# A streaming mean reduction: the first tile loaded by two DMAs, split by partitions

## The chip, the cores and the metric

The kernel runs on one core of one Trainium2 chip. The metric is the device time of one execution in microseconds. Every execution quoted here was with a granted clock of 1.00. Executions of one kernel agree within about 0.1%, so a difference of 1 us in 1246 can be read from medians, and one of 0.2 us can't.

Three words are used throughout. A *tile* is 8 MB of the input, 128 partitions with 65,536 bytes each. A *row* is the 65,536 bytes of one partition; in the trace it is one packet of one of the core's 16 DMA engines. A *piece* is one of the two DMAs that load the first tile after the change.

## The reference

```python
def setup_inputs():
    return {"x": np.random.randn(64, 256, 8192).astype(np.float32)}

def reference(x):
    return np.mean(x, axis=2)
```

That is 537 MB of input, read once, and 64 KB of output. The arithmetic is one addition for each element.

## The kernel before

The input is 16,384 vectors of 8192 floats. Two of them go to one partition and make a row in the sense above (the expectations below call the same thing, as it is read from memory, a row pair). 63 tiles go through three buffers in turn; the rest is loaded as one half tile and four column chunks. SyncE issues all loads. It issues tile t only when VectorE has reduced tile t-3. The first three loads are moved ahead of the start barrier.

```python
R = 2; NP = 63; NBUF = 3; P = 128; L = 8192
x_pair = x_rows.rearrange("(t p r) l -> t p (r l)", p=P, r=R)
bufs = [E(nc.sbuf_tensor(f"buf{i}", [P, R * L], f32)) for i in range(NBUF)]
in_sems = [E(nc.semaphore(f"in_sem{i}")) for i in range(NBUF)]
# ... cut: small buffers, other semaphores
def sync_program(eng):
    for t in range(NP):
        if t >= NBUF:
            eng.wait_ge(dve_sem, t - NBUF + 1)
        eng.dma_start(bufs[t % NBUF][:], x_pair[t]).then_inc(in_sems[t % NBUF], 16)
    # ... cut: the half tile, four column chunks, the stores

def vector_program(eng):
    def pair(k, trip, dst):
        eng.wait_ge(in_sems[k], trip)
        eng.tensor_reduce(dst, bufs[k][:].rearrange("p (r l) -> p r l", r=R), X, ADD
        ).then_inc(dve_sem, 1)
    with eng.Fori(0, trips) as i:
        for k in range(NBUF):
            pair(k, 16 * i + 16, res[:, bass.ds(NBUF * i + k, 1), :])
    # ... cut: the last tiles, and the sums that end the kernel
```

Of the kernel before, what the change touches and what calls it, by code (L numbers as in the profile page):

```python
# [6 lines left out]
def bass_global_avg_pool_1d_kernel(  # L7
# [4 lines left out]
    P = 128  # L12
# [14 lines left out]
    NBUF = 3  # L27
# [14 lines left out]
    with ExitStack() as ctx:  # L42
        E = ctx.enter_context
        bufs = [E(nc.sbuf_tensor(f"buf{i}", [P, R * L], f32)) for i in range(NBUF)]
        res = E(nc.sbuf_tensor("res", [P, NP, R], f32))
        res1 = E(nc.sbuf_tensor("res1", [P, 2], f32))
        part = E(nc.sbuf_tensor("part", [P, 8], f32))
        fin = E(nc.sbuf_tensor("fin", [P, 32], f32))
        fint = E(nc.sbuf_tensor("fint", [P, 32], f32))
        ident = E(nc.sbuf_tensor("ident", [P, P], f32))  # L50
        outsb = E(nc.sbuf_tensor("outsb", [NP, P, R], f32))
        out1sb = E(nc.sbuf_tensor("out1sb", [1, P], f32))
        ps = [E(nc.psum_tensor(f"ps{r}", [NP, P], f32)) for r in range(R)]
        psone = E(nc.psum_tensor("psone", [1, P], f32))

        in_sems = [E(nc.semaphore(f"in_sem{i}")) for i in range(NBUF)]
        one_sem = E(nc.semaphore("one_sem"))
        ch_sems = [E(nc.semaphore(f"ch_sem{i}")) for i in range(NCH)]
        dve_sem = E(nc.semaphore("dve_sem"))
        act_sem = E(nc.semaphore("act_sem"))  # L60
        prep_sem = E(nc.semaphore("prep_sem"))
        pe_sem = E(nc.semaphore("pe_sem"))
        cp_sem = E(nc.semaphore("cp_sem"))
        fin_sem = E(nc.semaphore("fin_sem"))
        out_sems = [E(nc.semaphore(f"out_sem{i}")) for i in range(3)]

        b1 = NP % NBUF
        b2 = (NP + 1) % NBUF
        buf1 = bufs[b1]
        buf2 = bufs[b2]  # L70
        offs = [sum(CH[:i]) for i in range(NCH)]
        s0 = CH[0] // 2 - L // 64
        s1 = CH[1] // 2

        def gpsimd_program(eng):
            eng.memset(fin[:], 0.0).then_inc(prep_sem, 1)  # L76
            eng.memset(ident[:], 0.0).then_inc(prep_sem, 1)  # L77
            eng.wait_ge(prep_sem, 2)
            eng.affine_select(  # L79
                out=ident[:],  # L80
                in_=ident[:],
                compare_op=mybir.AluOpType.not_equal,
                fill=1.0,
                base=0,
                pattern=[[-1, P]],
                channel_multiplier=1,
            ).then_inc(prep_sem, 1)

        first = len(nc.main_func.blocks[0].instructions)

        def sync_program(eng):
            for t in range(NP):
                if t >= NBUF:
                    eng.wait_ge(dve_sem, t - NBUF + 1)
                eng.dma_start(bufs[t % NBUF][:], x_pair[t]).then_inc(in_sems[t % NBUF], 16)  # L95
            eng.wait_ge(dve_sem, NP - NBUF + 1)
            eng.dma_start(buf1[:, :L], x_one[T1]).then_inc(one_sem, 16)
            eng.wait_ge(dve_sem, NP - NBUF + 2)
            for c in range(NCH):
                sl = slice(offs[c], offs[c] + CH[c])  # L100
                eng.dma_start(buf2[:, sl], x_one[T2][:, sl]).then_inc(ch_sems[c], 16)  # L101

            eng.wait_ge(cp_sem, 2)
            eng.dma_start(out_pair[0:NP, :], outsb[:].rearrange("t p r -> t (p r)")).then_inc(
                out_sems[0], 16
            )
            eng.wait_ge(cp_sem, 3)
            eng.dma_start(out_one[T1 : T1 + 1, :], out1sb[:]).then_inc(out_sems[1], 16)
            eng.wait_ge(fin_sem, 3)
            eng.dma_start(out_q[4 * T2 : 4 * T2 + 4, :], fint[0:P:32, :]).then_inc(  # L110
                out_sems[2], 16
            )
            for s in out_sems:
                eng.wait_ge(s, 16)
# [6 lines that stand above are left out]
                eng.tensor_reduce(  # L121
                    dst, bufs[k][:].rearrange("p (r l) -> p r l", r=R), X, ADD
                ).then_inc(dve_sem, 1)

            trips = (NP - 1) // NBUF
            with eng.Fori(0, trips) as i:
                for k in range(NBUF):
                    pair(k, 16 * i + 16, res[:, bass.ds(NBUF * i + k, 1), :])
            for t in range(trips * NBUF, NP - 1):
                pair(t % NBUF, 16 * (t // NBUF + 1), res[:, t, :])  # L130
            t = NP - 1
            eng.wait_ge(in_sems[t % NBUF], 16 * (t // NBUF + 1))
            eng.tensor_reduce(res[:, t, 0:1], bufs[t % NBUF][:, :L], X, ADD).then_inc(dve_sem, 1)  # L133
            eng.wait_ge(one_sem, 16)
            eng.tensor_reduce(res1[:, 0:1], buf1[:, : L // 2], X, ADD).then_inc(dve_sem, 1)  # L135
            eng.wait_ge(ch_sems[0], 16)
            eng.tensor_reduce(part[:, 0:1], buf2[:, :s0], X, ADD).then_inc(dve_sem, 1)  # L137
            eng.wait_ge(ch_sems[1], 16)
            eng.tensor_reduce(  # L139
                part[:, 1:2], buf2[:, offs[1] : offs[1] + s1], X, ADD  # L140
            ).then_inc(dve_sem, 1)
            eng.wait_ge(ch_sems[3], 16)
            eng.tensor_reduce(  # L143
                part[:, 2:3], buf2[:, offs[3] : offs[3] + CH[3]], X, ADD
            ).then_inc(dve_sem, 1)
            eng.wait_ge(dve_sem, NP + 4)
            eng.wait_ge(act_sem, 5)
            eng.wait_ge(prep_sem, 1)
            eng.tensor_reduce(fin[:, 0:1], part[:, 0:6], X, ADD).then_inc(fin_sem, 1)  # L149
            eng.wait_ge(fin_sem, 1)  # L150
            eng.transpose(fint[:], fin[:]).then_inc(fin_sem, 1)  # L151
            eng.wait_ge(fin_sem, 2)
            eng.tensor_scalar(  # L153
                fint[:], fint[:], inv, None, mybir.AluOpType.mult
            ).then_inc(fin_sem, 1)

        def scalar_program(eng):
            def acc(dst, src):
                eng.activation(src, src, Copy, accum_out=dst).then_inc(act_sem, 1)  # L159

            t = NP - 1
            eng.wait_ge(in_sems[t % NBUF], 16 * (t // NBUF + 1))
            acc(res[:, t, 1:2], bufs[t % NBUF][:, L:])
            eng.wait_ge(one_sem, 16)
            acc(res1[:, 1:2], buf1[:, L // 2 : L])

            for r in range(R):
                eng.wait_ge(pe_sem, r + 1)
                eng.activation(outsb[:, :, r], ps[r][:], Copy, scale=inv).then_inc(cp_sem, 1)  # L169
            eng.wait_ge(pe_sem, 3)  # L170
            eng.activation(out1sb[:], psone[:], Copy, scale=inv).then_inc(cp_sem, 1)  # L171
            eng.wait_ge(ch_sems[0], 16)
            acc(part[:, 3:4], buf2[:, s0 : CH[0]])
            eng.wait_ge(ch_sems[1], 16)
            acc(part[:, 4:5], buf2[:, offs[1] + s1 : offs[1] + CH[1]])
            eng.wait_ge(ch_sems[2], 16)
            acc(part[:, 5:6], buf2[:, offs[2] : offs[2] + CH[2]])

        def tensor_program(eng):
            eng.wait_ge(prep_sem, 3)  # L180
            eng.wait_ge(dve_sem, NP)
            eng.wait_ge(act_sem, 1)
            for r in range(R):
                eng.transpose(ps[r][:], res[:, :, r], ident[:]).then_inc(pe_sem, 1)  # L184
            eng.wait_ge(dve_sem, NP + 1)
            eng.wait_ge(act_sem, 2)
            eng.matmul(psone[:], res1[:, 0:1], ident[:], start=True, stop=False)  # L187
            eng.matmul(psone[:], res1[:, 1:2], ident[:], start=False, stop=True).then_inc(pe_sem, 1)  # L188

        sync_program(nc.sync)  # L190
        gpsimd_program(nc.gpsimd)
        vector_program(nc.vector)
        scalar_program(nc.scalar)
        tensor_program(nc.tensor)



        stream = nc.main_func.blocks[0].instructions
        loads = stream[first : first + NBUF]
        del stream[first : first + NBUF]  # L200
        at = next(
            i
            for i, ins in enumerate(stream)
            if ins.engine == mybir.EngineType.SP and type(ins).__name__ == "InstDrain"
        )
        stream[at:at] = loads
# [28 lines left out]
```

## Time and profile before

| | before |
|---|---|
| time, median of 3 | 1246.21 us (1245.99 to 1246.72) |
| DMA engines busy | 99.8% of the span |
| rate over the span | 431 GB/s |
| VectorE busy | 87% |
| one reduction of a tile | 17.22 us |
| one row on one DMA engine | 2.418 us, which is 27.1 GB/s |

These lines are from the page of the kernel before: the span; the busy share of the DMA engines in 40 slices, in tenths; what they moved in each slice; the DMA queue with packets, MB and share of 16 engines; the shares of the chain that ended last; and the costliest group of instructions, with its busy time, the mean of one in ns, and the idle time before it.

```profile
span 1244.7 us, 315 instructions
...
DMA  9999999999999999999999999999999999999998
GB/s 436 415 430 438 438 438 438 430 413 438 438 438 438 438 436 411 434 438 438 438 438 438 425 417 438 438 438 438 438 432 411 438 438 438 438 438 436 417 428 373
...
q1 hardware_dynamic: 9874, 536.94, 99.8%
...
DMA 70%; DVE 29%; issue 0%; SPq 0%; DVEq 0%
...
L121 DVE TENSOR_REDUCE res<-buf 128x16384 f32 (+1 forms) x62 | 1067.6, 17220 | 152.3 <-DMA buf<-in_x_dram 152.3
```

The DMA engines are busy 99.8% of the span, and VectorE waits 152.3 us in total for landings. The chain of work that ended last names VectorE for 29%, because each load is issued when a reduction ends, but in that wait the engines have other loads queued and stay busy (99.8%). Two lines of the timeline of VectorE before show the rhythm (start, duration, instruction, and in brackets the idle time before it and what ended it):

```profile
22.14 17.22 DVE L121 TENSOR_REDUCE res<-buf 128x16384 f32 x1 [22.14 <-DMA buf<-in_x_dram]
41.46 17.22 DVE L121 TENSOR_REDUCE res<-buf 128x16384 f32 x1 [2.10 <-DMA buf<-in_x_dram]
```

A tile arrives every 19.3 us, and VectorE is done with the last one 2.1 us earlier. When reduction t ends and tile t+3 is issued, the engines still have 2 us of tile t+1 and all of tile t+2 before them, about 21 us of queued work.

The packets of the trace can be joined into chains, because on each engine a packet starts where the one before ended. Before the change there are 16 such chains. They start between 1.04 and 1.94 us. Their first rows take 2.55 to 3.20 us, and after that practically every full row takes 2.42 us.

### The profile page before, as it was taken

Reading aid. Unit: us, or ns where it says so; the run is one execution under the profiler, and the core shown is the slowest. Engines: PE = TensorE matmul, PEld = TensorE weight load, DVE = VectorE, ACT = ScalarE, POOL = GpSimd, SP = SyncE. Lnnn points to the kernel's source line nnn. Section 1 sums busy time; section 2 is a strip of 40 time slices with the busy share of each in tenths; the row PEclk is TensorE's granted clock in tenths of the full one; section 3 lists DMA queues with packets and bytes.
Section 4 is the critical chain, followed back from the end, with each engine's and each line's share of the span. In section 5 each row is a group of like instructions: output and inputs, shape, how many; then the busy total and the mean of one; then the engine's idle time right before and its main releaser. Section 6 shows DMA issues by size and latency. Waiting matters only on the chain.

```text
span 1244.7 us, 315 instructions
## 1 busy us (share of the span) xinstructions
PE 1.7 (0%) x6; PEld 0.6 (0%) x6; DVE 1085.6 (87%) x70; ACT 17.2 (1%) x14; POOL 0.8 (0%) x7
## 2 busy tenths in 40 slices
PE   0000000000000000000000000000000000000000
PEld 0000000000000000000000000000000000000000
DVE  2898988989889889898898988989889898898897
ACT  0000000000000000000000000000000000000005
POOL 0000000000000000000000000000000000000000
DMA  9999999999999999999999999999999999999998
GB/s 436 415 430 438 438 438 438 430 413 438 438 438 438 438 436 411 434 438 438 438 438 438 425 417 438 438 438 438 438 432 411 438 438 438 438 438 436 417 428 373
DMA packets 9874, 536.94 MB, mean 431 GB/s; under 512 B 1106, under 2 KB 1170, under 8 KB 1426
## 3 DMA queue, kind: packets, MB, share of 16 engines
q1 hardware_dynamic: 9874, 536.94, 99.8%
HBM read 536.87 MB, written 0.07 MB: 431 GB/s over the span
## 4 chain that ended last, share of the span: by engine, by line
DMA 70%; DVE 29%; issue 0%; SPq 0%; DVEq 0%
DMA buf<-in_x_dram 70%; DVE res L121 29%; DVEq L121 0%; SPq L101 0%; DVE part L143 0%; SPq L95 0%; DVE fint L151 0%; DVE fint L153 0%; DVE fin L149 0%
## 5 line engine op out<-in xcount | busy, mean ns | idle before, releaser
L121 DVE TENSOR_REDUCE res<-buf 128x16384 f32 (+1 forms) x62 | 1067.6, 17220 | 152.3 <-DMA buf<-in_x_dram 152.3
L159 ACT ACTIVATE buf<-buf 128x1024 f32<-128x1024 f32 (+3 forms) x5 | 15.0, 2994 | 1221.7 <-DMA buf<-in_x_dram 1221.6
L133 DVE TENSOR_REDUCE res<-buf 128x1 f32<-128x8192 f32 x1 | 8.7, 8685 | 2.1 <-DMA buf<-in_x_dram 2.1
L135 DVE TENSOR_REDUCE res<-buf 128x1 f32<-128x4096 f32 x1 | 4.4, 4419 | 1.0 <-DMA buf<-in_x_dram 1.0
L137 DVE TENSOR_REDUCE part<-buf 128x1 f32<-128x2176 f32 x1 | 2.4, 2421 | 1.1 <-DMA buf<-in_x_dram 1.1
L184 PE MATMUL ps<-ident,res 128*63 128x128 f32 x2 | 0.7, 434 | 1230.8 <-DVE res L133 1230.8
L159 ACT ACT_TABLE_LOAD x1 | 1.3, 1283 | 1.8 <-PEq L220 1.8
L143 DVE TENSOR_REDUCE part<-buf 128x1 f32<-128x512 f32 x1 | 0.7, 686 | 0.7 <-DMA buf<-in_x_dram 0.7
L139 DVE TENSOR_REDUCE part<-buf 128x1 f32<-128x1024 f32 x1 | 1.2, 1220 | 0.1
L159 ACT ACTIVATION_READ_ACCUMULATOR buf<-buf 128x1 f32 x5 | 0.9, 186 | 0.0
L184 PEld LDWEIGHTS ps<-ident,res 128*63 128x63 f32 x2 | 0.3, 202 | 1230.8 <-issue 1230.8
L188 PE MATMUL psone<-ident,res 128*1 128x128 f32 x2 | 0.6, 421 | 0.0
L187 PE MATMUL psone<-ident,res 128*1 128x128 f32 x2 | 0.6, 397 | 4.7 <-DVE res L135 4.7
L169 ACT ACTIVATE outsb<-ps 63x128 f32<-63x128 f32 x2 | 0.4, 264 | 0.0
L79 POOL TENSOR_SCALAR_AFFINE_SELECT ident<-ident 128x128 f32<-128x128 f32 x1 | 0.3, 292 | 0.2 <-POOL ident L77 0.2
L171 ACT ACTIVATE out1sb<-psone 1x128 f32<-1x128 f32 x1 | 0.3, 266 | 1.5 <-PE psone L188 1.5
L188 PEld LDWEIGHTS psone<-ident,res 128*1 128x1 f32 x2 | 0.3, 128 | 0.2
L151 DVE STREAM_TRANSPOSE fint<-fin 128x32 f32<-128x32 f32 x1 | 0.2, 212 | 0.0
L153 DVE TENSOR_SCALAR fint<-fint 128x32 f32<-128x32 f32 x1 | 0.2, 181 | 0.0
L77 POOL MEMSET ident<- 128x128 f32 x1 | 0.2, 204 | 0.0
L149 DVE TENSOR_REDUCE fin<-part 128x1 f32<-128x6 f32 x1 | 0.2, 159 | 0.0
L76 POOL MEMSET fin<- 128x32 f32 x1 | 0.1, 125 | 1.3 <-POOLq L220 1.3
(5 smaller groups left out, 0.5 us busy)
## 6 DMA issues: line engine op xcount, KB each, us to landing
buf<-in_x_dram SPq DMA_DIRECT2D x1, 4096.0 KB, 31.1
buf<-in_x_dram SPq DMA_DIRECT2D x1, 2304.0 KB, 17.3
buf<-in_x_dram SPq DMA_DIRECT2D x1, 1024.0 KB, 19.4
buf<-in_x_dram SPq DMA_DIRECT2D x63, 40.7
buf<-in_x_dram SPq DMA_DIRECT2D x1, 512.0 KB, 20.2
buf<-in_x_dram SPq DMA_DIRECT2D x1, 256.0 KB, 20.4
out_dram<-outsb SPq DMA_DIRECT2D x1, 63.0 KB
out_dram<-out1sb SPq DMA_DIRECT2D x1, 0.5 KB
```

The costliest lines, as they stand in the source:

```text
L79: eng.affine_select(out=ident[:], in_=ident[:], compare_op=mybir.AluOpType.not_equal, fill=1.0, base=0, pattern=[[-1, P]], channel_multipl ...
L121: eng.tensor_reduce(dst, bufs[k][:].rearrange("p (r l) -> p r l", r=R), X, ADD).then_inc(dve_sem, 1)
L133: eng.tensor_reduce(res[:, t, 0:1], bufs[t % NBUF][:, :L], X, ADD).then_inc(dve_sem, 1)
L135: eng.tensor_reduce(res1[:, 0:1], buf1[:, : L // 2], X, ADD).then_inc(dve_sem, 1)
L137: eng.tensor_reduce(part[:, 0:1], buf2[:, :s0], X, ADD).then_inc(dve_sem, 1)
L139: eng.tensor_reduce(part[:, 1:2], buf2[:, offs[1] : offs[1] + s1], X, ADD).then_inc(dve_sem, 1)
L143: eng.tensor_reduce(part[:, 2:3], buf2[:, offs[3] : offs[3] + CH[3]], X, ADD).then_inc(dve_sem, 1)
L159: eng.activation(src, src, Copy, accum_out=dst).then_inc(act_sem, 1)
L169: eng.activation(outsb[:, :, r], ps[r][:], Copy, scale=inv).then_inc(cp_sem, 1)
L184: eng.transpose(ps[r][:], res[:, :, r], ident[:]).then_inc(pe_sem, 1)
L187: eng.matmul(psone[:], res1[:, 0:1], ident[:], start=True, stop=False)
L188: eng.matmul(psone[:], res1[:, 1:2], ident[:], start=False, stop=True).then_inc(pe_sem, 1)
```

## The change

The intent: a small first DMA might get the engines going sooner than one over 128 partitions. The first tile is loaded as partitions 0 to 15 (1 MB) and then 16 to 127 (7 MB). Both pieces count up the same semaphore, so the waits on buffer 0 ask for 16 more.

```diff
+        def landed(t):
+            return 16 * (t // NBUF + 1 + (t % NBUF == 0))
...
-                eng.dma_start(bufs[t % NBUF][:], x_pair[t]).then_inc(in_sems[t % NBUF], 16)
+                for ps in (slice(0, 16), slice(16, P)) if t == 0 else (slice(0, P),):
+                    eng.dma_start(bufs[t % NBUF][ps], x_pair[t][ps]).then_inc(
+                        in_sems[t % NBUF], 16
+                    )
...
-                    pair(k, 16 * i + 16, res[:, bass.ds(NBUF * i + k, 1), :])
+                    pair(k, 16 * i + landed(k), res[:, bass.ds(NBUF * i + k, 1), :])
...  (the other waits on in_sems likewise; NBUF + 1 loads are moved ahead of the barrier)
```

More of the change, by code (lines that the diff above doesn't have):

```diff
@@ L127, in vector_program @@
                 for k in range(NBUF):
-                    pair(k, 16 * i + 16, res[:, bass.ds(NBUF * i + k, 1), :])
+                    pair(k, 16 * i + landed(k), res[:, bass.ds(NBUF * i + k, 1), :])
             for t in range(trips * NBUF, NP - 1):
-                pair(t % NBUF, 16 * (t // NBUF + 1), res[:, t, :])
+                pair(t % NBUF, landed(t), res[:, t, :])
             t = NP - 1
-            eng.wait_ge(in_sems[t % NBUF], 16 * (t // NBUF + 1))
+            eng.wait_ge(in_sems[t % NBUF], landed(t))
             eng.tensor_reduce(res[:, t, 0:1], bufs[t % NBUF][:, :L], X, ADD).then_inc(dve_sem, 1)
@@ L161, in scalar_program @@
             t = NP - 1
-            eng.wait_ge(in_sems[t % NBUF], 16 * (t // NBUF + 1))
+            eng.wait_ge(in_sems[t % NBUF], landed(t))
             acc(res[:, t, 1:2], bufs[t % NBUF][:, L:])
@@ L198, in bass_global_avg_pool_1d_kernel @@
         stream = nc.main_func.blocks[0].instructions
-        loads = stream[first : first + NBUF]
-        del stream[first : first + NBUF]
+        loads = stream[first : first + NBUF + 1]
+        del stream[first : first + NBUF + 1]
         at = next(
```

## The prediction

> **What bounds it now.** The load stream. The page gives DMA 99.8% busy over 16 engines and 431 GB/s over the 1244.7 us span; DVE is busy 87% and waits for landings. In the packets of the trace a full row (65,536 B) takes 2.418 us on an engine (27.1 GB/s), and each engine's next packet starts when its last ends: 16 unbroken chains from 1.04-1.94 us (first packets, 2.5 to 3.2 us each) to the last load's semaphore at 1241.6 us. An 8 MB tile is 8 rows per engine, 19.3 us. A tile's reduction takes 17.22 us. The issue of tile t+3 comes at the end of reduction t, about 2 us before tile t+1 lands, with all of tile t+2 queued: about 21 us of slack. So only time lost or saved by the slowest DMA engine counts, and it counts one for one.
>
> **What the change adds and removes.** It adds one DMA issue (0.41 us each at the start, hidden behind rows of 2.4 us), a register instruction per trip of DVE's loop (DVE waits about 2 us per tile: free) and a wait for 32 instead of 16. Its hope is that a 16-row DMA starts the engines sooner: the first packets start over 0.9 us, so at most that can be won, more likely 0 to 0.5 us.
>
> **The cost I expect.** [...] both pieces still use 16 engines: 16 = 16x1 rows, 112 = 16x7. [...] The trace before has only 128-partition loads, each engine at its full rate, so no run here shows this yet. [...] With jitter in the starts, both pieces together cost the slowest engine 13 to 18 us.
> [...]
>
> Tile 0 lands at about 37 us instead of 22 us. Its reduction and the issue of tile 3 come about 15 us later, inside the 21 us of slack, so nothing starves; but the lost DMA time is never won back. The whole loss is on the critical path.
>
> **Prediction.** 1260 us, 80% range 1250 to 1270. Faster by over 2%: 0.01; within 2%: 0.87; slower by over 2%: 0.12.
>
> **What would show it.** First-row packets of about 9 to 10 us instead of 3; packets of 2.4 to 10 us in the second piece; 2.418 us rows from tile 1 on; DVE's first wait about 37 us instead of 22.1; low GB/s in the first of the 40 slices; steady period unchanged at 19.35 us; the landings of one tile spread over several us (0.75 us before), lasting to the end; the DMA share below 99.8% or unchanged with longer packets.
>
> **What would make it wrong.** [...] a landing later than the 21 us of slack: up to some 1275. Skew between engines that makes later tiles collide would cost more.

The forecast's sum came to 13 to 18 us for both pieces on the slowest engine, and so from the 1246 us of before to 1260 us. The terms of that sum, one for each piece, rested on a model of how the partitions of a piece slow its rows, which no trace or run shows.

## The result, and the profile after

| | before | after |
|---|---|---|
| time, median of 4 | 1246.31 us | 1267.28 us (1266.93 to 1268.19) |
| ratio, after over before | | 1.0169 (95% interval 1.0152 to 1.0187) |
| first reduction starts | 22.14 us | 44.49 us |
| mean rate | 431 GB/s | 424 GB/s |
| DMA engines busy | 99.8% | 99.7% |

Ratios here are the mean time of one kernel's fast runs over that of the other's of the same rounds, so not quite the ratio of the medians that are quoted. The change costs 21 us, 1.7%, clear of noise. The profiled execution was the slowest of the four (1268.19 us), and its span is 22.1 us longer than that of before (1266.8 against 1244.7); the decomposition below belongs to it.

The page after:

```profile
span 1266.8 us, 336 instructions
...
DMA  9999999999999999999999999999999999999997
GB/s 223 348 441 437 433 433 430 430 430 430 430 433 441 445 433 433 433 430 430 430 430 430 435 439 447 430 435 430 430 430 430 430 430 433 445 443 430 435 430 337
...
q1 hardware_dynamic: 9890, 536.94, 99.7%
...
L128 DVE TENSOR_REDUCE res<-buf 128x16384 f32 (+1 forms) x62 | 1067.6, 17220 | 174.4 <-DMA buf<-in_x_dram 174.4
```

The busy digits are as before. What is new is in the line of GB/s: 223 and 348 in the first two slices. The engines read as busy and moved half of what they had moved before in the first slice, and some four fifths in the second. VectorE's reductions take what they took, and its idle time is 22.1 us longer (174.4 against 152.3), which is the whole difference of the spans. Its timeline after shows that all of it is one wait:

```profile
44.49 17.22 DVE L128 TENSOR_REDUCE res<-buf 128x16384 f32 x1 [44.49 <-DMA buf<-in_x_dram]
63.83 17.22 DVE L128 TENSOR_REDUCE res<-buf 128x16384 f32 x1 [2.11 <-DMA buf<-in_x_dram]
83.18 17.22 DVE L128 TENSOR_REDUCE res<-buf 128x16384 f32 x1 [2.13 <-DMA buf<-in_x_dram]
```

The same three stretches of both kernels follow, first before and then after (the stretch in us; busy time of PE, PEld, DVE, ACT and POOL with counts of instructions; the clock; the share of the DMA engines; GB/s). A packet counts where it starts, so a share can pass 1.

```profile
1.00:12.00 11.00, 0.00 (x0) 0.00 (x0) 0.00 (x0) 1.28 (x1) 0.56 (x3) 1.00 1.15 477
12.00:44.00 32.00, 0.00 (x0) 0.00 (x0) 19.76 (x2) 0.00 (x0) 0.00 (x0) 1.00 0.98 426
44.00:64.00 20.00, 0.00 (x0) 0.00 (x0) 17.86 (x2) 0.00 (x0) 0.00 (x0) 1.00 0.97 419
```

```profile
1.00:12.00 11.00, 0.00 (x0) 0.00 (x0) 0.00 (x0) 1.28 (x1) 0.56 (x3) 1.00 1.28 191
12.00:44.00 32.00, 0.00 (x0) 0.00 (x0) 0.00 (x0) 0.00 (x0) 0.00 (x0) 1.00 0.93 238
44.00:64.00 20.00, 0.00 (x0) 0.00 (x0) 17.39 (x2) 0.00 (x0) 0.00 (x0) 1.00 1.04 449
```

The rate falls to 191 and 238 GB/s and is back in the third stretch. Because a packet counts where it starts, these figures are too high for the pieces themselves: the first stretch also counts the first rows of piece 2, and the second counts rows of tile 1. From the starts and ends of the rows below, piece 1 moved its 1 MB in 9.4 us, which is 111 GB/s, and piece 2 its 112 rows in 32.8 us, 224 GB/s. The rows themselves, from the packets of the trace, joined into one chain for each engine (durations in us over the 16 engines; "last end" is when the last engine ended that row):

```
                  before                          after
row of the chain  min  median  max   last end     min  median  max   last end
1                 2.55  3.06  3.20     4.74       7.92  8.66  9.16    10.44   piece 1
2                 2.42  2.42  2.42     7.16       5.22  5.31  5.89    15.66   piece 2
3                 2.42  2.42  2.42     9.57       4.71  4.72  4.80    20.37
4                 2.42  2.42  2.42    11.99       2.96  3.07  4.84    25.20
5                 2.42  2.42  2.42    14.41       3.62  3.62  4.48    28.94
6                 2.42  2.42  2.42    16.82       4.29  4.57  4.76    33.63
7                 2.42  2.42  2.42    19.24       4.70  4.76  4.87    38.38
8                 2.42  2.42  2.42    21.66       4.52  4.57  4.89    43.26
9 (tile 1)        2.42  2.42  2.42    24.08       2.82  3.39  3.67    46.20
```

The sum closes. After piece 1 the last engine is 5.7 us behind (10.44 - 4.74). Piece 2 adds 15.9 us (43.26 - 10.44 is 32.8 us, against 21.66 - 4.74 = 16.9). The first row of tile 1 adds 0.5 us (2.94 against 2.42). 5.7 + 15.9 + 0.5 = 22.1 us, the difference of the spans. The engines started as they had before, at 1.02 to 1.82 us, so the hoped-for gain is not there. From row 10 on every row takes 2.42 us in the median again.

### The profile page after: what moved, and what is told of

It reads as the page before. It is cut to its first block, busy times and chain, and to the rows that moved or that the text cites. A ratio compares the mean times of both kernels' runs of the same rounds, so it can differ in the third digit from the quotient of the medians.

```text
span 1266.8 us, 336 instructions
## 1 busy us (share of the span) xinstructions
PE 1.7 (0%) x6; PEld 0.6 (0%) x6; DVE 1085.6 (86%) x70; ACT 17.2 (1%) x14; POOL 0.8 (0%) x7
## 3 DMA queue, kind: packets, MB, share of 16 engines
q1 hardware_dynamic: 9890, 536.94, 99.7%
## 4 chain that ended last, share of the span: by engine, by line
DMA 69%; DVE 29%; another core or an unknown queue 2%; issue 0%; SPq 0%; DVEq 0%
DMA buf<-in_x_dram 69%; DVE res L128 29%; DVEq L128 0%; SPq L108 0%; DVE part L150 0%; SPq L100 0%; DVE fint L158 0%; DVE fint L160 0%; DVE fin L156 0%
## 5 line engine op out<-in xcount | busy, mean ns | idle before, releaser
L128 DVE TENSOR_REDUCE res<-buf 128x16384 f32 (+1 forms) x62 | 1067.6, 17220 | 174.4 <-DMA buf<-in_x_dram 174.4
```

## The experiments

The theory (A): which partitions a load writes sets how long its rows take. Over all 128 partitions a row takes 2.42 us; in piece 1 of the change it took 8.66 us in the median, in piece 2 from 3.07 to 5.31. In its plain form A says that only the rows that get in each other's way are slow; in the form A2 they hold up the other engines too. The sizes that the expectations give for A come from an estimate; its terms no run here shows. The rivals: a second DMA costs this whatever its shape (B); only the start of the program is sensitive (C); the addresses read in HBM do it, not the partitions written (D); any load below 128 partitions is slow (E).

All runs gave correct results. The median differences below are against the kernel before in the same rounds.

### 1. Two DMAs, split by columns

```diff
-                for ps in (slice(0, 16), slice(16, P)) if t == 0 else (slice(0, P),):
-                    eng.dma_start(bufs[t % NBUF][ps], x_pair[t][ps]).then_inc(
+                for cs in (slice(0, 2048), slice(2048, R * L)) if t == 0 else (slice(0, R * L),):
+                    eng.dma_start(bufs[t % NBUF][:, cs], x_pair[t][:, cs]).then_inc(
```

> The first tile is again loaded by two DMAs of 1 MB and 7 MB with the same semaphore counts, but both cover all 128 partitions: columns 0 to 2047 and then 2048 to 16383. Theory A [...]: no loss, 1245.8 to 1246.8 us, rows of tile 1 at 2.42 us as before, landing of tile 0 near 22 us. Rival B (a second DMA, its issue, the doubled semaphore count or the later loop register work costs the 21 us, whatever the shape): 1262 us or more, tile 0 landing near 44 us.

Measured: 1245.89 us against 1246.07, ratio 0.9998 (0.9985 to 1.0012). VectorE's timeline in this run starts as before:

```profile
22.19 17.22 DVE L128 TENSOR_REDUCE res<-buf 128x16384 f32 x1 [22.19 <-DMA buf<-in_x_dram]
41.54 17.22 DVE L128 TENSOR_REDUCE res<-buf 128x16384 f32 x1 [2.13 <-DMA buf<-in_x_dram]
```

The same two sizes, the same extra issue, the same semaphore counts and the same code on VectorE, and no loss. (The packets differ: one of piece 1 is 8 KB here, as each partition gets 2048 floats; the page counts 10018 in all, against 9874 before.) B falls. This is also the repair: a load that must be split can be split by columns.

### 2. The same split, at tile 60

```diff
-                for ps in (slice(0, 16), slice(16, P)) if t == 0 else (slice(0, P),):
+                for ps in (slice(0, 16), slice(16, P)) if t == 60 else (slice(0, P),):
-            return 16 * (t // NBUF + 1 + (t % NBUF == 0))
+            return 16 * (t // NBUF + 1 + (t == 60))
...  (cut: three loads instead of four are moved ahead of the barrier)
```

> Tile 0 is loaded whole; tile 60 is loaded as partitions 0 to 15 and then 16 to 127. Theory A [...]: about the same loss as at tile 0, 1263 to 1268 us, with rows slowed only in tile 60. Rival C (the loss belongs to the start: a cold DMA queue, or VectorE starting 22 us later and never catching up): below 1250 us, because DVE has nothing to start late for there.

Measured: 1268.85 us, 22.8 us over before (ratio 1.018), slightly above the range expected. The wait is now late in VectorE's timeline, 23.55 us before tile 60, and 1.5 us more than usual before tile 59, which landed while the small piece of tile 60 was being loaded:

```profile
1145.24 17.22 DVE L128 TENSOR_REDUCE res<-buf 128x16384 f32 x1 [2.13 <-DMA buf<-in_x_dram]
1166.03 17.22 DVE L128 TENSOR_REDUCE res<-buf 128x16384 f32 x1 [3.58 <-DMA buf<-in_x_dram]
1206.81 17.22 DVE L128 TENSOR_REDUCE res<-buf 128x2 f32<-128x16384 f32 x1 [23.55 <-DMA buf<-in_x_dram]
```

The rows of that tile repeat the pattern of the change: 8.64, 5.29, 4.78, 2.94, 4.11, 4.57, 4.76, 4.39 us in the median. C falls. VectorE's late start at tile 0 is a sign of the loss and not its cause.

### 3. Two halves of 64 partitions

```diff
-                for ps in (slice(0, 16), slice(16, P)) if t == 0 else (slice(0, P),):
+                for ps in (slice(0, 64), slice(64, P)) if t == 0 else (slice(0, P),):
```

> The first tile as two DMAs of 64 partitions. Theory A [...] rows of 4.84 us, loss 18.5 to 20 us: 1265 to 1267 us. [...] If a piece of 64 partitions were spread well: 1246 us.

Measured: 1267.01 us, 20.9 us over before (ratio 1.0167). Both halves have all 16 engines at 5.1 us a row (5.12 in the median; 4.70 and 4.93 for the first rows of the two halves). The direction is as A says, and the size a little over its range, because a row took 2.12 times the 2.418 us of a load over 128 partitions, where the expectation had twice (4.84 us). 16 rows in 5.12 us are 205 GB/s.

### 4. Eight pieces of 16 partitions

```diff
-                for ps in (slice(0, 16), slice(16, P)) if t == 0 else (slice(0, P),):
+                for ps in [slice(q, q + 16) for q in range(0, P, 16)] if t == 0 else (slice(0, P),):
-            return 16 * (t // NBUF + 1 + (t % NBUF == 0))
+            return 16 * (t // NBUF + 1 + 7 * (t % NBUF == 0))
...  (cut: ten loads instead of four are moved ahead of the barrier)
```

> The first tile as eight DMAs of 16 partitions each. Theory A: one row for each engine in each piece[...], 1289 to 1304 us, slower by over 2%. Rival B (a price for each additional DMA): seven times the loss of one more DMA, some 147 us. Rival C (only a cold first DMA): about as the change, 1267 us or less.

Measured: 1301.07 us, 55.0 us over before (ratio 1.0442, slower by over 2%). Rows 2 to 8 of all 16 engines take 9.33 us. From the page of this run, what was moved in each of the 40 slices:

```profile
DMA  9899999999999999999999999999999999999998
GB/s 129 97 323 452 420 450 422 422 450 420 452 420 450 422 424 448 420 452 420 450 422 428 444 420 452 420 450 422 430 442 420 452 420 452 420 432 440 420 452 357
```

The DMA engines read as busy as ever, at 129 and 97 GB/s. Seven more DMAs cost neither seven times the 21 us (B) nor nothing (C). So a row took 2.42 us in loads over 128 partitions, 5.12 us in pieces of 64 neighbouring partitions and 9.33 us in pieces of 16 such: 2.12 and 3.86 times as long. 16 rows in 9.33 us are 112 GB/s.

### 5 and 6. One extra load of 1 MB: 16 rows, or the same bytes over 128 partitions

To weigh piece 1 by itself, a load of 1 MB is added at the head of the queue, into buffer 2. The real load of tile 2 waits for it and overwrites it, so the result stays right. The tiles are loaded whole, as before the change.

```diff
+            eng.dma_start(bufs[2][0:16], x_pair[2][0:16]).then_inc(ext_sem, 16)
             for t in range(NP):
+                if t == 2:
+                    eng.wait_ge(ext_sem, 16)
```

> All tiles are loaded whole; one extra load of 1 MB, rows of tile 2 into partitions 0 to 15 of its buffer, goes first in the queue (the real load of tile 2 waits for it and overwrites it). Theory A: [...] the row takes 8 to 9.7 us instead of 2.4 to 3, so the time grows by about 8 to 9.5 us, to 1254 to 1256 us. [...]

The control, with `[:, 0:2048]` for `[0:16]` on both sides:

> The control: an extra load of the same 1 MB and at the same place, as columns 0 to 2047 of all 128 partitions. All theories: only its bytes, 2.4 us at 27.1 GB/s an engine, so 1248.3 to 1249.2 us.

Measured: 1255.22 us with 16 rows and 1248.81 us with columns, against 1246.45: 8.8 and 2.4 us. The columns cost their bytes and nothing more. The 16 rows took 7.65 to 9.07 us. Writing to partitions 0 to 15 cost 8.8 - 2.4 = 6.4 us more than the bytes, which agrees with the 5.7 us of piece 1 within a microsecond.

### 7. The extra 1 MB into every eighth partition

```diff
-            eng.dma_start(bufs[2][0:16], x_pair[2][0:16]).then_inc(ext_sem, 16)
+            eng.dma_start(bufs[2][0:128:8], x_pair[2][0:128:8]).then_inc(ext_sem, 16)
```

> The same extra 1 MB into 16 partitions, but every eighth one (0, 8, ... 120). Theory A [...] the row takes about 4.8 us, time plus 4.4 to 5.4 us, 1250.5 to 1252 us. If what counts is the number of partitions and not which: as with partitions 0 to 15, 1254 to 1256 us.

Measured: 1251.06 us, 4.6 us over before; rows of 4.30 to 5.55 us, median 4.86. The number of partitions is the same as in run 5, and the price beyond that of the bytes falls from 6.4 to 2.2 us (4.6 - 2.4). So it counts which partitions they are, and not only how many. E would fit this run too, as these rows are slower than 2.42 us as well; see run 12.

### 9 and 10. Read side or write side

In runs 5 and 7 the rows read are spread in the same way as the partitions written. Here one is changed without the other. Into partitions 0 to 15 from every eighth row pair:

```diff
-            eng.dma_start(bufs[2][0:16], x_pair[2][0:16]).then_inc(ext_sem, 16)
+            eng.dma_start(bufs[2][0:16], x_pair[2][0:128:8]).then_inc(ext_sem, 16)
```

> As the extra 1 MB into partitions 0 to 15 (1255.2 us, first rows 7.7 to 9.1 us), but read from every eighth row pair of the source. [...] (theory A): the same 1254.5 to 1256 us, rows near 8.5 us. If the read side decides (rival D, addresses that lie close together in HBM): as the run into every eighth partition, about 1251 us, rows near 4.9 us.

Into every eighth partition from neighbouring row pairs, with `bufs[2][0:128:8], x_pair[2][0:16]`:

> The other half of the crossing: the extra 1 MB is read from the 16 neighbouring row pairs and written to every eighth partition. Theory A: 1250.5 to 1251.5 us, rows near 4.9 us. Rival D: 1254.5 to 1256 us, rows near 8.5 us.

Measured, with the times over before and the median row:

```
                         read from neighbours     read from every 8th
written to 0 to 15       +8.8 us, row 8.49        +8.7 us, row 8.62
written to every 8th     +4.8 us, row 4.60        +4.6 us, row 4.86
```

Of the two, only the partitions written matter. D falls for these sets of partitions.

### 8. Two rows, into partitions 0 and 1

```diff
-            eng.dma_start(bufs[2][0:16], x_pair[2][0:16]).then_inc(ext_sem, 16)
+            eng.dma_start(bufs[2][0:2], x_pair[2][0:2]).then_inc(ext_sem, 16)
```

> The extra load is two rows only (128 KB), partitions 0 and 1: two engines with one row each[...]. Theory A [...]: those two rows take 4.8 us, every other engine goes on with rows of 2.42 us; the slowest engine loses about 4.4 to 4.8 us, 1250.5 to 1251.2 us. Theory A2 [...]: the same total or a little more, but the first rows of the other 14 engines are also well over 3.2 us.

Measured: 1249.56 us, 3.1 us over before, below what either form of the theory had said. Two chains have first rows of 4.17 and 4.37 us; the other 14 have 2.42 to 3.30 us. So only two rows are slow, as the plain form of A has it, and the first rows of the others show no slowing. The total was overestimated in part because the two rows took less than 4.8 us, and in part because these two engines started first (0.92 us, the last engine at 2.42) and so had a lead to lose.

### 11. The extra 1 MB into every seventh partition

The second piece of the change has 112 rows, seven for each engine. The model behind the prediction did not give what the table of rows shows: all 16 engines slow together, as at 4.71 to 4.80 us in row 3. This run takes 16 of the partitions of that piece.

```diff
-            eng.dma_start(bufs[2][0:16], x_pair[2][0:16]).then_inc(ext_sem, 16)
+            eng.dma_start(bufs[2][16:128:7], x_pair[2][16:128:7]).then_inc(ext_sem, 16)
```

> The extra 1 MB goes to every seventh partition from 16 (16, 23, ... 121)[...]. [...] (A): four engines with rows of 4.4 to 5 us, twelve with 2.5 to 3.3 us; total 1250 to 1251.5 us. Hold-up of the others (A2), which the 16 equally slow engines in the second piece suggest: all or nearly all 16 rows at 4 us or more, the same total. [...]

Measured: 1251.44 us, 5.1 us over before. All 16 rows take 4.03 to 5.22 us, 4.56 in the median. The total can't tell the two forms of the theory apart, because a few slow rows are enough to delay the slowest engine (two cost 3.1 us in run 8); the rows can. The plain form of A, with 2.5 to 3.3 us for twelve of them, fails here. A line of the windows of this run (the last number is GB/s):

```profile
1.00:10.00 9.00, 0.00 (x0) 0.00 (x0) 0.00 (x0) 1.28 (x1) 0.56 (x3) 1.00 1.10 350
```

### 12. The extra 1 MB into every fourth partition

If it counts which partitions are written and not how many, there may be 16 whose rows take no longer than in a load over 128. Steps of four from partition 32 were taken for such a set by an estimate that no earlier run shows.

```diff
-            eng.dma_start(bufs[2][0:16], x_pair[2][0:16]).then_inc(ext_sem, 16)
+            eng.dma_start(bufs[2][32:96:4], x_pair[2][32:96:4]).then_inc(ext_sem, 16)
```

> The extra 1 MB goes to partitions 32, 36, ... 92. [...] Theory A2 [...] rows of 2.5 to 3.3 us as in an ordinary first row and only the bytes' price, 1248.3 to 1249.3 us. Rival E (a DMA that covers fewer than 128 partitions is slow [...]): rows of 4 us or more, 1250.5 us or more[...].

Measured: 1248.74 us, 2.3 us over before, the price of the bytes and no more. The rows take 2.42 to 3.19 us, as first rows did before the change. The same stretch in the windows of this run (before the change it is also 466 GB/s):

```profile
1.00:10.00 9.00, 0.00 (x0) 0.00 (x0) 0.00 (x0) 1.28 (x1) 0.56 (x3) 1.00 1.13 466
```

E falls: a small number of partitions is not slow in itself.

With the same bytes and the same number of partitions, the cost of 1 MB is 8.8 us (partitions 0 to 15), 4.6 us (every eighth from 0), 5.1 us (every seventh from 16) or 2.3 us (every fourth from 32).

No version was found that beats the kernel before. Before the change, the engines already carry rows of 2.42 us from 1.0 us to the end, and the column split is equal to it within 0.2%.

## Why the prediction was right, point by point

- **What bounds the kernel, and that lost DMA time is not won back: right.** The difference of the spans is that of VectorE's one wait, and the later waits are 2.1 us as before. Run 2 shows the same loss (22.8 us) near the end of the stream.
- **No gain from the start: right.** The prediction allowed 0 to 0.5 us. The first packets start at 1.02 to 1.82 us instead of 1.04 to 1.94; nothing of it shows in the time.
- **Both pieces still use 16 engines: right.** There are 16 chains with eight rows each. 16 and 112 rows both went to 16 engines.
- **Piece 1: right in kind, 5.7 us in size.** The first rows were forecast at "about 9 to 10 us instead of 3" and took 7.92 to 9.16, 8.66 in the median. The first row of before took 3.06, since the first rows are longer there too (2.55 to 3.20 us against 2.42).
- **Piece 2: too small in the sum; it cost 15.9 us.** With the 5.7 us of piece 1 it makes 21.6 us, against 13 to 18 forecast for both. In rows 2, 3 and 6 to 8 of the change all 16 engines ran slow (4.29 to 5.89 us), and run 11, with 16 of the partitions of that piece, shows the same (4.03 to 5.22).
- **Tile 0 lands "at about 37 us": 44.4 us. "Inside the 21 us of slack": right that nothing starves, but for another reason.** Tile 3 was issued at 61.74 us instead of 39.39, over 22 us later, which is more than the slack, and no engine ran dry; the wait after the next landing was 2.11 us. The delay did not use up the slack, because it moved the queued loads as well: the last rows of tile 2 ended between 80.2 and 82.5 us instead of 59.6 and 60.3. From the issue of tile 3 to those ends it is 18 to 21 us after the change, and was 20 to 21 before. So the prediction's warning of a landing "later than the 21 us of slack" names a danger that was not there.
- **The landings of a tile spread over several us: right in direction.** The semaphore of tile 1 counts from 61.27 to 63.68 us, 2.4 us, instead of 0.7 us (40.61 to 41.32). It lasts to the end, as forecast: the last rows of tile 62 end over 2.4 us, and over 0.4 us before the change.
- **1260 us, range 1250 to 1270: 1267.28 is inside.** The middle missed by 7 us. The loss of 21 us is also more than the 13 to 18 us that the prediction had worked out for both pieces, so it was the margin of the range that took it in.

What stays open is why all 16 rows are slow in run 11 (4.03 to 5.22 us) and none in run 12 (2.42 to 3.19 us), while two slow rows in run 8 slowed nobody else. Two readings are left: some of the rows in run 11 hold up the others; or the reads, seven row pairs apart, have a part in it, since runs 9 and 10 crossed reads and writes for other sets only. The trace doesn't name the partition of a packet, so which engine writes which partition is not shown either, and no rule that gives the price of a set of partitions was shown. It leaves untouched what the runs do show: which partitions are written decides most of the price, and not the fact of a split, the start or the number of partitions, nor, in the sets that were crossed, the addresses read. It is shown best by run 5 against run 6, with the same bytes at the same place (8.8 against 2.4 us), and by run 5 against run 12, with the same number of partitions (8.8 against 2.3 us).

## What to carry to other kernels

When a load is split, split it along the free dimension and keep all 128 partitions in each piece: the column split cost nothing here (ratio 0.9998), the row splits cost 21 to 55 us for one tile in 64. If fewer partitions must be loaded, it matters which: the rows of 16 partitions in steps of seven took 4.03 to 5.22 us, and those in steps of four 2.42 to 3.19 us. A DMA share of 99% doesn't show this (99.7% after the change, with 223 GB/s in the first slice); look at GB/s by slice, and at how long packets of one size take.
